# Splitting the streamed weights of a hybrid layer by DMA instead of by ScalarE and VectorE

## The chip, the cores and the metric

The kernel runs on one NeuronCore of one Trainium2 chip. The metric is the device time of one execution in microseconds (us); the lower, the better. The kernel before takes 900.84 us, the median of 3 runs (900.33 to 902.33).

## The reference, cut to what matters

One decoder layer on 512 tokens of width 1024, all in float32: RMSNorm, one wide input projection, four mixer branches (a short gated convolution, causal pooling, a 31-tap convolution, differential attention), each gated by a sigmoid and summed, an output projection, and a gated feed-forward part of inner width 2816.

```python
h = rms_norm(x, mix_norm)
z = h @ w_in
sc_b, sc_c, sc_x, pool_in, conf_in, q, k, v, gate_logits = split(z)
y = [short_conv(...) @ sc_out, pool_mixer(...), conformer(...) @ conf_out, diff_attention(...) @ diff_out]
x = x + sum_i(sigmoid(gate_i) * y_i) @ w_o
h2 = rms_norm(x, ffn_norm)
u = causal_dwconv(h2 @ w_up, conv_w)          # 2 x 2816 channels
x = x + (silu(gate(u)) * up(u)) @ w_down
```

Nearly all the arithmetic is products of an activation with a weight, and each weight is used once, for all 512 tokens.

## The kernel before

**Precision.** TensorE multiplies in the type F32R, which keeps fewer bits than F32. So every operand is written as a pair: `hi`, the value rounded to F32R, and `lo = value - hi`, rounded too. `mm3` makes one product out of three matmuls (lines 134 to 136): hi with hi, hi of the first with lo of the second, lo of the first with hi of the second. In `project` the first is the weight.

**The stream of weights.** All weights lie in HBM as one array `w` of 155 chunks of 128 x 1024 F32 (512 KB) in the order in which they are used. A chunk holds 8 units, a unit being a 128 x 128 block. Each call of `unit` hands out the next unit, lets work run that was put off by so many units (`events`), and calls `load_chunk` until chunk c + AHEAD is there (AHEAD = 2).

**Loading a chunk.** `fetch` issues a DMA on SP's queue into `raw`, of which there are two buffers. Then ScalarE copies `raw` to `hi` with a cast (L108) and VectorE subtracts `hi` from `raw` into `lo` (L109). There are three buffers each of `hi` (`whi`) and `lo` (`wlo`). A buffer comes free when the last matmul that reads it is done. The first chunk is split in 4 pieces, the second in 2.

**Order.** The program is written with tiles, and a planner puts the instructions of each engine in order: of those whose inputs it reckons ready it takes the one written first. Each engine, and each queue that issues DMAs, then works strictly in the order given, and an instruction that waits holds up those behind it. Only for the first two chunks is the order of ScalarE and VectorE the written one (`manual_schedule`).

**The other work.** GpSimd sums squares of the input (L207), raises to the power -1/2 (L249, L348), clears the padding of tiles (L85) and adds up the pooling windows (L491). It issues no DMA. VectorE and ScalarE do all that reads PSUM: norms, convolutions, softmax, gates, and the split of activations. Eight PSUM banks hold the results of the projections until then. `at_` are two buffers of the attention part, used again by the feed-forward part.

Of the kernel before, what the change touches and what calls it, by code (L numbers as in the profile page):

```python
# [9 lines left out]
F32 = mybir.dt.float32  # L10
F32R = mybir.dt.float32r
AF = mybir.ActivationFunctionType
ALU = mybir.AluOpType
AX = mybir.AxisListType

P = 128
T = 512
# [10 lines left out]
CW = 1024  # L28
TW = T + CK - 1
UPC = CW // P  # L30
AHEAD = 2
STEP = 13
TAP0 = 32
TAP1 = 560
# [8 lines left out]
HP = 0  # L43
# [20 lines left out]
def hybrid_layer_kernel(ctx: ExitStack, tc: tile.TileContext, xT: bass.AP, w: bass.AP, cols: bass.AP, out: bass.AP):  # L64
    nc = tc.nc
    const = ctx.enter_context(tc.tile_pool(name="const", bufs=1))
    big = ctx.enter_context(tc.tile_pool(name="big", bufs=1))
    wp = ctx.enter_context(tc.tile_pool(name="wp", bufs=3))
# [19 lines left out]
    chunks = []  # L88
# [2 lines left out]
    early = []  # L91

    def fetch(c, pieces=1):
        raw = wp.tile([P, CW], F32, tag="raw", name=f"wr{c}", bufs=2)
        for i in range(pieces):
            s = slice(i * CW // pieces, (i + 1) * CW // pieces)
            nc.sync.dma_start(raw[:, s], w[c][:, s])
        return raw

    def load_chunk(pieces=1):  # L100
        c = len(chunks)
        raw = early.pop(0) if early else fetch(c)
        hi = wp.tile([P, CW], F32R, tag="whi", name=f"wh{c}", bufs=3)
        lo = wp.tile([P, CW], F32R, tag="wlo", name=f"wl{c}", bufs=3)
        with tc.high_priority(HP):
            for i in range(pieces):
                s = slice(i * CW // pieces, (i + 1) * CW // pieces)
                nc.scalar.copy(hi[:, s], raw[:, s])  # L108
                nc.vector.tensor_tensor(out=lo[:, s], in0=raw[:, s], in1=hi[:, s].bitcast(F32), op=ALU.subtract)  # L109
        chunks.append((hi, lo))  # L110
# [11 lines left out]
    def unit(width=1):  # L122
        u = state["unit"]
        state["unit"] += width
        while events and events[0][0] <= u:
            events.pop(0)[2]()
        c, o = divmod(u, UPC)
        while len(chunks) <= min(c + AHEAD, n_chunks - 1):
            load_chunk()
        s = slice(o * P, (o + width) * P)  # L130
        return chunks[c][0][:, s], chunks[c][1][:, s]
# [48 lines left out]
    nc.scalar.copy(ones, ones32)  # L180
    xin = [big.tile([P, 4, T], F32, tag=f"od{i}", name=f"xin{i}") for i in range(2)]
    hs = big.tile([P, KD, 2, T], F32R, name="hs")
    at_ = [big.tile([P, 4, T], F32R, name=f"at{i}") for i in range(2)]
    xt = [xin[k // 4][:, k % 4, :] for k in range(KD)]
    raw = []
    total = const.tile([P, T], F32, name="total")
# [4 lines left out]
    nc.sync.dma_start(xt[0], xT[0])  # L191
    nc.sync.dma_start(gains, cols[:, :NG])
    early.append(fetch(0, 2))
    nc.sync.dma_start(xt[1], xT[1])
    early.append(fetch(1))
    nc.sync.dma_start(xin[0][:, 2:4, :], xT[2:4].rearrange("k p t -> p k t"))
    nc.sync.dma_start(xin[1], xT[4:8].rearrange("k p t -> p k t"))
# [11 lines left out]
    with tc.manual_schedule(engines={mybir.EngineType.Activation, mybir.EngineType.DVE}):  # L209
        raw_in(0)  # L210
        load_chunk(PIECES)
        raw_in(1)
        load_chunk(2)
        for k in range(2):
            add_square(total, xt[k], k == 0, f"sq{k}", nc.gpsimd)
# [179 lines left out]
    nc.scalar.activation(lam2, lam2, AF.Exp)  # L395
    nc.vector.tensor_tensor(out=lam, in0=lam2[:, 0:1], in1=lam2[:, 1:2], op=ALU.subtract)
    nc.vector.tensor_scalar(out=lam, in0=lam, scalar1=LAM_INIT, scalar2=None, op0=ALU.add)

    def scores(i, hd):
        n = (i + 1) * P  # L400
        qs = slice(i * P, n)
        sc = [bank(f"sc{i}{hd}{m}") for m in range(2)]
        for a, b, s0, s1 in ((0, 0, True, False), (0, 1, False, False), (1, 0, False, True)):
            for m in range(2):
                r = slice(m * HD, (m + 1) * HD)
                nc.tensor.matmul(sc[m][:, :n], qT[hd][a][r, qs], kT[hd][b][r, :n], start=s0, stop=s1)
        st = sm.tile([P, 4], F32, tag="st", name=f"st{i}{hd}")
        ps = []
        for m in range(2):
            p = t2(f"p{i}{hd}{m}")  # L410
            nc.vector.tensor_tensor_reduce(  # L411
                out=p[:, :n], in0=sc[m][:, :n], in1=mask[:, T - n:], scale=-1.0, scalar=-NEG, op0=ALU.add, op1=ALU.min,
                accum_out=st[:, m:m + 1])
            nc.scalar.activation(  # L414
                p[:, :n], p[:, :n], AF.Exp, bias=st[:, m:m + 1], scale=-1.0, accum_out=st[:, 2 + m:3 + m])
            ps.append(p)
        nc.vector.reciprocal(st[:, 2:4], st[:, 2:4])
        nc.vector.tensor_tensor(out=st[:, 3:4], in0=st[:, 3:4], in1=lam, op=ALU.mult)
        nc.scalar.activation(ps[1][:, :n], ps[1][:, :n], AF.Copy, scale=st[:, 3:4])
        nc.vector.scalar_tensor_tensor(  # L420
            out=ps[0][:, :n], in0=ps[0][:, :n], scalar=st[:, 2:3], in1=ps[1][:, :n],
            op0=ALU.mult, op1=ALU.subtract)
        after(LAG, lambda: values(i, hd, ps[0]))
# [307 lines left out]
```

## Time and profile before

| what | value |
|---|---|
| runs, median (lowest to highest) | 900.84 us (900.33 to 902.33) |
| profiled execution, first to last instruction | 899.2 us |
| PE busy | 890.3 us, 99% |
| PEld (weight loads) busy | 725.8 us, 81% |
| VectorE (DVE) busy | 592.2 us, 66% |
| ScalarE (ACT) busy | 387.3 us, 43% |
| GpSimd (POOL) busy | 47.9 us, 5% |
| HBM read | 85.75 MB, 98 GB/s with what is written |

For the profiled execution the profile gives the span, not a time of its own beside it: 899.2 us from the first to the last instruction, 1.6 us under the median of the runs. That difference is taken as what lies around the span. Matmuls are pipelined, so how close PE is to its limit is read from the distance between the starts of its matmuls and not from its busy share.

### The profile page before, as it was taken

How to read it: one execution, taken by the hardware profiler on the slowest of the kernel's cores; microseconds unless marked ns; L12 is line 12 of the kernel's file. 1: busy time of each engine (PE TensorE's matmuls, PEld its weight loads, DVE VectorE, ACT ScalarE, POOL GpSimd, SP SyncE). 2: the span in 40 equal slices, each digit the busy share in tenths (PEclk: the TensorE clock that was granted, in tenths of full speed). 3: DMA queues.
4: the chain of work that ended last, by engine and by line, in shares of the span. 5: the costliest groups of instructions: out<-in, count | busy, mean ns of one | idle time of the engine just before them, and what ended most of it. 6: DMA issues, size and time to landing. Idle time of an engine off the chain costs nothing.

```text
span 899.2 us, 10320 instructions
## 1 busy us (share of the span) xinstructions
PE 890.3 (99%) x3974; PEld 725.8 (81%) x3974; DVE 592.2 (66%) x853; ACT 387.3 (43%) x544; POOL 47.9 (5%) x108
## 2 busy tenths in 40 slices
PE   7999999999999999999999999999999999999998
PEld 5888887778787888888888888888888888888886
DVE  6599855998575999743558555877777777632221
ACT  6333454464588352222574346444444444311110
POOL 5003300002400000000000000000000000000000
PEclk9999999999999999999999999999999999999999
DMA  5423222222132222222334332322223322233330
GB/s 199 141 90 99 71 93 94 71 71 95 47 110 78 94 94 94 93 94 94 96 96 159 135 99 72 117 94 95 94 94 101 107 97 94 94 117 106 117 105 24
DMA packets 26337, 88.51 MB, mean 98 GB/s; under 512 B 2992, under 2 KB 3248, under 8 KB 26288
## 3 DMA queue, kind: packets, MB, share of 16 engines
q1 hardware_dynamic: 26288, 87.86, 29.3%
q8 instruction: 31, 0.51, 0.2%
q14 instruction: 18, 0.15, 0.1%
HBM read 85.75 MB, written 2.10 MB: 98 GB/s over the span
## 4 chain that ended last, share of the span: by engine, by line
PE 92%; DVE 4%; ACT 2%; issue 1%; DMA 1%; SPq 0%; DVEq 0%; ACTq 0%
PE dn L135 4%; PE dn L136 4%; PE dn L134 4%; PE fg L134 4%; PE fu L134 4%; PE fg L136 4%; PE fu L136 4%; PE fg L135 4%; PE fu L135 4%; PE gts L134 2%; PE wo L134 2%; PE wo L136 2%; PE wo L135 2%; PE gts L135 2%; PE gts L136 2%; PE gtp L134 2%
## 5 line engine op out<-in xcount | busy, mean ns | idle before, releaser
L109 DVE TENSOR_TENSOR wl<-wr,wh 128x1024 fp32r<-128x1024 f32 (+1 forms) x159 | 192.8, 1216 | 134.5 <-ACT wh L108 126.9
L108 ACT CAST wh<-wr 128x1024 fp32r<-128x1024 f32 (+1 forms) x159 | 163.3, 1030 | 261.9 <-PE dn L135 80.2
L324 DVE SCALAR_TENSOR_TENSOR cacc<-glu,colt,cacc 128x512 f32<-128x512 f32 x120 | 89.2, 755 | 1.6
L134 PE MATMUL fg<-hs,wh 128*128 128x512 f32 x176 | 68.5, 389 | 0.0
L136 PE MATMUL fg<-hs,wl 128*128 128x512 f32 x176 | 68.5, 389 | 0.0
L136 PE MATMUL fu<-hs,wl 128*128 128x512 f32 x176 | 68.5, 389 | 0.0
L135 PE MATMUL fg<-hs,wh 128*128 128x512 f32 x176 | 68.5, 389 | 0.0
L134 PE MATMUL fu<-hs,wh 128*128 128x512 f32 x176 | 68.5, 389 | 0.0
L135 PE MATMUL fu<-hs,wh 128*128 128x512 f32 x176 | 68.5, 389 | 0.0
L611 DVE SCALAR_TENSOR_TENSOR fc<-f,colt,fc 128x512 f32<-128x512 f32 x88 | 65.8, 749 | 1.4
L136 PEld LDWEIGHTS fu<-hs,wl 128*128 128x128 f32 x176 | 33.1, 188 | 6.9
L134 PEld LDWEIGHTS fg<-hs,wh 128*128 128x128 f32 x176 | 33.1, 188 | 6.9
L135 PEld LDWEIGHTS fu<-hs,wh 128*128 128x128 f32 x176 | 33.0, 188 | 6.9
L136 PEld LDWEIGHTS fg<-hs,wl 128*128 128x128 f32 x176 | 33.0, 187 | 6.9
L135 PEld LDWEIGHTS fg<-hs,wh 128*128 128x128 f32 x176 | 33.0, 188 | 6.8
L134 PEld LDWEIGHTS fu<-hs,wh 128*128 128x128 f32 x176 | 33.0, 187 | 6.8
L606 DVE TENSOR_TENSOR f<-fu,rs 128x512 f32<-128x512 f32 x22 | 15.2, 692 | 34.5 <-PE fu L136 34.5
L609 ACT ACTIVATE fc<-f,colt 128x512 f32<-128x512 f32 x44 | 31.9, 726 | 4.8 <-DVE f L606 4.6
L85 POOL MEMSET f<- 128x2 f32 x44 | 4.4, 100 | 507.1 <-DVE total L207 292.7
L624 ACT ACTIVATE fc<-fc 128x512 f32<-128x512 f32 x22 | 13.9, 634 | 38.7 <-DVE fc L611 38.7
L414 ACT ACTIVATE p<-p,st 128x128 f32<-128x128 f32 (+3 forms) x32 | 17.8, 556 | 29.6 <-DVE st L411 29.6
L134 PE MATMUL gts<-hs,wh 128*128 128x512 f32 x64 | 26.0, 406 | 0.0
(920 smaller groups left out, 2099.6 us busy)
## 6 DMA issues: line engine op xcount, KB each, us to landing
wr<-w SPq DMA_DIRECT2D x154, 512.0 KB, 3.3
x<-xT SPq DMA_DIRECT2D x8, 256.0 KB, 5.0
outT<-out SPq DMA_DIRECT2D x7, 256.0 KB, 2.6
xin<-xT SPq DMA_DIRECT2D x1, 1024.0 KB, 9.2
xin<-xT SPq DMA_DIRECT2D x2, 256.0 KB, 4.0
wr<-w SPq DMA_DIRECT2D x2, 256.0 KB, 3.7
xin<-xT SPq DMA_DIRECT2D x1, 512.0 KB, 7.0
colt<-cols SPq DMA_DIRECT2D x1, 273.5 KB, 9.4
```

Of the source, the lines that this page charges most:

```text
L85: nc.gpsimd.memset(t[:, :n], 0.0)
L108: nc.scalar.copy(hi[:, s], raw[:, s])
L109: nc.vector.tensor_tensor(out=lo[:, s], in0=raw[:, s], in1=hi[:, s].bitcast(F32), op=ALU.subtract)
L134: nc.tensor.matmul(ps, a[0], b[0], start=start, stop=False)
L135: nc.tensor.matmul(ps, a[0], b[1], start=False, stop=False)
L136: nc.tensor.matmul(ps, a[1], b[0], start=False, stop=stop)
L324: nc.vector.scalar_tensor_tensor(out=acc31[j], in0=glus[j][:, i:i + T], scalar=wc, in1=acc31[j], op0=ALU.mult, op1=ALU.add)
L414: nc.scalar.activation(p[:, :n], p[:, :n], AF.Exp, bias=st[:, m:m + 1], scale=-1.0, accum_out=st[:, 2 + m:3 + m])
L606: nc.vector.tensor_tensor(out=u[:, 2:2 + T], in0=ps, in1=rs, op=ALU.mult)
L609: nc.scalar.activation(c, u[:, 2:2 + T], AF.Copy, scale=col("ffn_conv", o + 2))
L611: nc.vector.scalar_tensor_tensor(out=c, in0=u[:, i:i + T], scalar=col("ffn_conv", o + i), in1=c, op0=ALU.mult, op1=ALU.add)
L624: nc.scalar.activation(g, g, AF.Silu)
```

## The change

Chunks 0 to 3 are loaded as before. From chunk 4 on (`ENGINES = 4`) three steps make the pair, without a raw copy in SBUF:

- a DMA issued by GpSimd writes the chunk from HBM into `hi`, with a cast to F32R on the way;
- ScalarE writes `-hi` into the tile `lo`;
- a second DMA issued by GpSimd reads the chunk from HBM again and adds it onto `lo`.

AHEAD becomes 3, and there are four buffers each of `hi` and `lo`. The `raw` buffers of the first four chunks lie in the memory of `at_`, which is allocated later.

```diff
-AHEAD = 2
+AHEAD = 3
+ENGINES = 4
...
     def fetch(c, pieces=1):
-        raw = wp.tile([P, CW], F32, tag="raw", name=f"wr{c}", bufs=2)
+        raw = big.tile([P, 2, CW], F32, tag=f"at{c % 2}", name=f"wr{c}")[:, 0, :]
...
+    def weight_pair(c):
+        return tuple(wp.tile([P, CW], F32R, tag=f"w{x}", name=f"w{x[0]}{c}", bufs=4) for x in ("hi", "lo"))
+
+    def split_by_dma(c):
+        hi, lo = weight_pair(c)
+        nc.gpsimd.dma_start(hi, w[c])
+        with tc.high_priority(HP):
+            nc.scalar.activation(lo, hi.bitcast(F32), AF.Copy, scale=-1.0)
+        nc.gpsimd.dma_start(lo, w[c], accum_op=ALU.add)
+        return hi, lo
+
     def load_chunk(pieces=1):
         c = len(chunks)
+        if c >= ENGINES:
+            chunks.append(split_by_dma(c))
+            return
         raw = early.pop(0) if early else fetch(c)
-        hi = wp.tile([P, CW], F32R, tag="whi", name=f"wh{c}", bufs=3)
-        lo = wp.tile([P, CW], F32R, tag="wlo", name=f"wl{c}", bufs=3)
+        hi, lo = weight_pair(c)
...
-    at_ = [big.tile([P, 4, T], F32R, name=f"at{i}") for i in range(2)]
...
+    at_ = [big.tile([P, 4, T], F32R, tag=f"at{i}", name=f"at{i}") for i in range(2)]
```

The pair holds the same values in both kernels, up to the rounding of the last step.

## Rows read from the trace of the kernel before

**Rows 1.** Page, part 1: busy us (share of the span) x instructions.

```profile
PE 890.3 (99%) x3974; PEld 725.8 (81%) x3974; DVE 592.2 (66%) x853; ACT 387.3 (43%) x544; POOL 47.9 (5%) x108
```

**Rows 2.** Waits of PE: for what, us in total, times, longest us.

```profile
PE ca L136 <- DVE wl L109: 2.8, 1, 2.8
PE warm L202 <- DVE zeros L199: 1.4, 1, 1.4
PE ca L134 <- ACT wh L108: 0.5, 1, 0.5
PE os L450 <- DVE oq1l L160: 0.2, 1, 0.2
```

**Rows 3.** Timeline of PE in the feed-forward part, eight units apart: start, duration, instruction.

```profile
599.63 0.39 PE L134 MATMUL fu<-hs,wh 128*128 128x512 f32 x1
...
605.07 0.39 PE L134 MATMUL fg<-hs,wh 128*128 128x512 f32 x1
```

**Rows 4.** Timeline of PE: a gap, chunk 4's first; chain of waits: the last add.

```profile
19.24 0.40 PE L135 MATMUL ca<-raw4l,wh 128*128 128x512 f32 x1
22.41 0.96 PE L136 MATMUL ca<-raw4h,wl 128*128 128x512 f32 x3 [2.77 <-DVE wl L109]
...
33.12 0.48 PE L134 MATMUL pa<-raw0h,wh 128*128 128x512 f32 x1
...
895.42 0.42 DVE out L636
```

**Rows 5.** Page, part 5, the split of weights: busy us, mean ns, idle before.

```profile
L109 DVE TENSOR_TENSOR wl<-wr,wh 128x1024 fp32r<-128x1024 f32 (+1 forms) x159 | 192.8, 1216 | 134.5 <-ACT wh L108 126.9
L108 ACT CAST wh<-wr 128x1024 fp32r<-128x1024 f32 (+1 forms) x159 | 163.3, 1030 | 261.9 <-PE dn L135 80.2
```

**Rows 6.** The line of the chunks' DMAs: issue ns min/median/max, and time to landing.

```profile
L97 SPq DMA_DIRECT2D wr<-w x156: 327/328/432, 1.6 to 870.1; - x156
...
DMA to landing us min/median/max: 3.0/3.3/8.1
```

**Rows 7.** Page, part 3: SP's queue: packets, MB, share of 16 engines' span.

```profile
q1 hardware_dynamic: 26288, 87.86, 29.3%
```

**Rows 8.** Waits of SP's queue, the longest.

```profile
SPq L97 <- DVE wl L109: 737.9, 147, 13.4
```

**Rows 9.** GpSimd's instructions by line: busy us, mean ns, idle before.

```profile
L348 POOL TENSOR_TENSOR qss<-qss,half 128x8 f32<-128x8 f32 x4 | 7.3, 1853 | 44.8 <-DVE qss L346 44.8
...
L249 POOL TENSOR_TENSOR r1r<-r1v,half 128x4 f32<-128x4 f32 x1 | 1.0, 1020 | 10.0 <-DVE r1v L247 10.0
```

**Rows 10.** GpSimd's timeline: two rows of the start, two of the pooling part.

```profile
0.87 0.10 POOL L221 MEMSET epsc<- 128x1 f32 x1
...
11.47 12.02 POOL L207 TENSOR_TENSOR total<-total,sq 128x512 f32<-128x512 f32 x7 [8.51 <-ACT sq L205]
...
210.89 1.62 POOL L491 TENSOR_TENSOR ps<-px 128x527 f32<-128x527 f32 x1 [13.15 <-ACT px L486]
...
235.65 4.07 POOL L491 TENSOR_TENSOR ps<-ps 128x525 f32<-128x525 f32 x3
```

**Rows 11.** Waits of ACT from 130 to 310 us, the longest.

```profile
ACT p L414 <- DVE st L411: 29.6, 14, 4.7
```

**Rows 12.** By stretch: busy us (x) of PE, PEld, DVE, ACT, POOL; clock; DMA share; GB/s.

```profile
130.00:200.00 70.00, 70.00 (x331) 55.44 (x329) 53.05 (x107) 35.95 (x69) 0.31 (x3) 1.00 0.24 83
200.00:240.00 40.00, 39.74 (x191) 31.18 (x190) 30.99 (x59) 17.59 (x35) 13.78 (x13) 1.00 0.25 79
...
500.00:750.00 250.00, 250.00 (x1102) 206.41 (x1101) 179.60 (x228) 115.03 (x147) 4.31 (x43) 1.00 0.29 97
780.00:880.00 100.00, 100.00 (x438) 81.96 (x438) 26.60 (x26) 19.86 (x19) 0.00 (x0) 1.00 0.31 106
```

## The prediction

> **What bounds the kernel now.** I read the busy shares first: PE is busy for 890.3 of 899.2 us, VectorE for two thirds, GpSimd for 5% [rows 1]. Since matmuls overlap, the share alone proves little, so I went on to the starts. In the feed-forward part eight units, that is one chunk or 24 matmuls, start from 599.63 to 605.07: 5.44 us, 0.227 us a matmul, with no gap [rows 3]. The waits of PE are the third view: 2.8 us for the low part of a chunk, 1.4 us before the warm-up, 0.5 and 0.2 us, 4.9 us in all [rows 2]. So PE sets the pace from end to end, and nearly nothing waits ahead of it. The granted clock is full (1.00, the 2.4 GHz level) in every stretch shown [rows 12]. From the first matmul of chunk 4 at 33.12 to the last output add at 895.42 [rows 4] are 862.3 us for the 151 chunks that the change touches: 5.71 us a chunk on average, 5.44 where PE does nothing else.
>
> The reader should see from this that the change works on engines that don't set the time. It can win a few us where PE waits, and it loses whatever its new chain fails to deliver every 5.44 us.
>
> **What is removed.** VectorE loses 151 subtractions of 1.216 us, 184 us of its 592 [rows 1, 5]. PE waits for one of these in a place that matters, once, for 2.8 us [rows 2], and that one belongs to chunk 2 (raw4 is unit 16 and up), which VectorE still splits. So this is worth 0 on the path; what hides it is PE's own work. SP loses 151 issues of 0.33 us [rows 6], and its wait for VectorE to free `raw` (737.9 us in all [rows 8]), also worth 0, since chunks lie ready ahead of PE. ScalarE keeps one pass over each chunk. I price the negation as the cast it replaces, 1.03 us [rows 5]: 0 again.
>
> **What is added.** Per chunk GpSimd issues two DMAs. Before, it issues none, so three prices aren't in the trace.
>
> - *The issue itself.* From below SP's issue, 0.33 us [rows 6]; from above GpSimd's dearest small instruction, 1.85 us, with 1.02 for the cheapest that computes [rows 9]. I take 1.0, that of a small program on the engine that has to do it. Two per chunk are 2.0 us of 5.44, beside 48 us of other work in the whole kernel [rows 1]. From either end the engine fits (0.7 to 3.7 us a chunk).
> - *The casting DMA.* SP's queue moved 87.86 MB in 29.3% of 899.2 us on all 16 engines [rows 7]: 263 us, 3.0 us per MB, 1.57 us for a chunk of 0.524 MB. That is my price if the cast is free; nothing cheaper is possible for the same bytes. From above, the worst landing of a chunk, 8.1 us [rows 6].
> - *The accumulating DMA.* It has to fetch the old content of `lo` besides the weight, so two reads for each write. From below again 1.57 us, from above 8.1. I take twice the copy, 3.1 us, as reads set the pace if both come through the same engine.
>
> The Trainium skill says the same of a DMA that adds ("Collectives: The Full Stack", section "The bandwidth ceiling: the fold count and why AG ≠ RS ≠ AR"): it needs two source reads and runs at half the rate of a copy. No row here shows it; an estimate by that page is 3.1 us too.
>
> The sum per chunk on the DMA engines is 1.57 + 3.1 = 4.7 us of 5.44, 86% in the dense stretches, where it was 0.29 to 0.31 before [rows 12]. It fits, with 0.8 us to spare: this is the tightest place of the whole change. From the bounds it is 3.1 to 16.2 us a chunk.
>
> **The latency of a chunk.** With four buffers, chunk c + 4 takes the place of c, so its first DMA waits until PE has read c for the last time, and PE needs c + 4 three chunks later, after 3 x 5.44 = 16.3 us. The chain in between: issue 1.0, landing 3.3 [rows 6], ScalarE 1.03 after whatever stands before it, issue 1.0, landing 3.3 plus the 1.57 that the second read adds: 11.2 us. That leaves 5.1 us. In the score stage ScalarE stands still up to 4.7 us for VectorE, 14 times [rows 11], and GpSimd has a block of 4.07 us of pooling sums and a wait of 13.15 us before another [rows 10]; each alone fits barely or falls into the planner's order.
>
> **What else waits on GpSimd.** The adds of the input norm (11.5 to 23.5 us), the powers, the paddings and the pooling sums now stand in one queue with DMAs that wait for PE or ScalarE. The adds end 9.6 us before chunk 4 starts [rows 4, 10], and the paddings are asked for well before PE would run out of its eight banks. I cost this at 0; without the cover it is some us per place.
>
> **The start.** Chunks 2 and 3 are still split by the engines, and the 2.8 us gap before 22.41 [rows 4] is VectorE finishing chunk 2 behind the splits of the input. AHEAD = 3 only brings chunk 3 forward. I take 0; the bounds are -2.8 (gap closed) and +2.8 (chunk 3 taking VectorE's time from the input in the same way).
>
> **The sum.** 899.2 us of span, plus 0 for PE's work, 0 for VectorE, SP and ScalarE, 0 at the start, plus the 1.6 us by which the median of the runs lies over the span: 900.8 us. Differences under 0.2% (1.8 us) can't be told from no change in this kernel.
>
> **The rivals.** Each steady rival has a lap time p per chunk, and from rows 4 the total is 33.1 + 151 p + 3.8 + 1.6 = 38.5 + 151 p; p = 5.71 gives back 900.7.
>
> - *The DMA engines become the bound.* If the cast isn't free, or the add costs over 2.5 copies, the two transfers exceed 5.44 us. With three copies' worth p is 1.57 + 4.7 = 6.3 and the time 990 us; it decides from 3.87 us for the add on. For it: 86% by my own sum, and no row of such a DMA. Against: 3.0 us per MB is a price from engines that were idle for 70% of the time [rows 7]; with more queued they may move more per us. Chance 0.24.
> - *GpSimd's queue turns latency into pace.* A strict order cast, add, cast, add makes each cast wait until ScalarE has negated the chunk before. The planner does reorder GpSimd: the padding constant of L221 ran at 0.87 us, before the add of L207 that is written earlier and ran at 11.47 [rows 10]. But by rows the add is ready 3.3 + 1.03 = 4.3 us after the cast, sooner than the next buffer comes free (5.44), so the planner may well choose just that order. The lap is then 4.3 plus an issue of 0.33 to 1.0, 4.7 to 5.4 us, if the add of the chunk before leaves the engines free, and up to 3.1 more if it doesn't: 8.5. Halfway, p = 6.6 and 1035 us. It decides from a lap of 5.44. Chance 0.18. The Trainium skill speaks against the change here ("DMA: Bandwidth & Descriptors", section "Latency and other measured facts"): a DMA generated in software on GpSimd delivers its first byte after about 1 us, one generated in hardware after about 0.6. No row here shows the former; an estimate with 0.4 us more is p = 7.0 and 1095 us.
> - *Local stalls.* Where ScalarE's waits of up to 4.7 us and GpSimd's blocks of 4 meet the 5.1 us to spare, from about 30 to 310 us, PE waits now and then. Two to five times some 2 to 4 us is +4 to +20, about 911 us. Chance 0.16.
> - *Faster.* The gap at the start closes, since the planner places the chunks anew: 900.8 - 2.8 = 898.0 us. For it: it is the one wait of size that PE has. Against: the chunk concerned is split as before. Chance 0.12.
>
> **How the numbers follow.** That the new chain keeps up and nothing changes has 0.30, the largest single chance, so the predicted time is 900.8 us, with 899.0 to 902.6 as its own range. Faster has 0.12, and slower 0.24 + 0.18 + 0.16 = 0.58, spread over three mechanisms with different times. The range of 8 in 10 goes from 897 to 1060 us: no change and faster (0.41 of 0.42), local stalls (0.16), about 0.15 of the DMA bound (p up to 6.77) and half of the queue's (0.08), 0.80 in all.
>
> **What the profile after would show.** If I am right, PE's waits stay near 5 us, matmuls start every 0.227 us, VectorE is near 408 us busy, the DMA share is 0.8 or more in the feed-forward part, and the casts are issued as soon as PE frees a buffer. A DMA share at 1.0 with PE waiting for the add shows the first rival; PE waiting at a DMA share well under 1, with GpSimd's queue alternating strictly and waiting for ScalarE, the second; waits of PE confined to the part before 310 us, the third. What would make the forecast wrong first is the price of the accumulating DMA, for which I have only the copy.

## The result, and the profile after

The changed kernel takes 1062.11 us (median of 4 runs, 1060.18 to 1065.03) where the kernel before takes 900.92: a ratio of 1.178, 95% interval 1.175 to 1.181. It is slower, and the forecast of 900.8 us is missed, also by the range, which ended at 1060.

The page of the profiled execution (span 1058.5 us), first its busy times, then its DMA queues and its issues with the median time to landing:

```profile
PE 942.4 (89%) x3974; PEld 744.1 (70%) x3974; DVE 419.4 (40%) x702; ACT 380.3 (36%) x544; POOL 259.8 (25%) x410
...
q0 software_dynamic: 43488, 158.35, 65.2%
q1 hardware_dynamic: 4544, 8.68, 2.3%
...
wh<-w POOLq DMA_DIRECT2D x151, 512.0 KB, 6.6
wl<-w POOLq DMA_DIRECT2D x151, 512.0 KB, 5.4
```

PE is idle for 116 us where it was idle for 9 [rows 1]. VectorE has lost 173 us of work, as the change says, and nothing comes of it. The DMA engines read nearly twice the bytes (164.9 MB, 85.75 before) and are still busy for only two thirds of the time, so they aren't full. GpSimd is at 25%, not full either. Where a kernel is slower by 18% and no engine is full, engines wait for each other, and the waits show which. Who waited for whom, us in total, times, longest:

```profile
POOL wl L109 <- ACT wl L108: 693.8, 137, 11.6
ACT wl L108 <- DMA wh<-w: 417.5, 94, 9.1
...
PE fu L150 <- DMA wl<-w: 18.1, 14, 3.0
PE dn L150 <- DMA wl<-w: 15.2, 8, 2.8
PE os L464 <- ACT oq1h L173: 8.5, 1, 8.5
```

L106 is the casting DMA, L108 ScalarE's negation, L109 the accumulating DMA. GpSimd stands at the add and waits for ScalarE, ScalarE waits for the cast to land, and PE waits for the add: 70 us of its waits are for `wl`, 42 for ScalarE and VectorE. The timeline of GpSimd, and then of ScalarE, over one turn of this circle (start, duration, instruction, idle time before it and its releaser):

```profile
179.29 0.85 POOL L109 DMA_DIRECT2D wl<-w  x1 [6.49 <-ACT wl L108]
179.84 0.87 POOL L106 DMA_DIRECT2D wh<-w  x1
180.38 0.44 POOL L86 MEMSET u<- 128x2 f32 x1
187.86 0.85 POOL L109 DMA_DIRECT2D wl<-w  x1 [7.04 <-ACT wl L108]
188.40 0.87 POOL L106 DMA_DIRECT2D wh<-w  x1
...
186.50 1.06 ACT L108 ACTIVATE wl<-wh 128x1024 fp32r<-128x1024 f32 x1 [4.45 <-DMA wh<-w]
```

The cast goes out at 179.84, right behind the add of the chunk before (179.29). The negation starts at 186.50, 6.66 us later, and takes 1.06. The add starts at 187.86 and the next cast at 188.40: 8.56 us from cast to cast, where PE uses up a chunk in 5.44 [rows 3]. The next cast stands behind the add in the queue, so it can't go out early although the DMA engines have room. In GpSimd's timeline this order, add of c ahead of the cast of c + 1, holds for 99 of the 150 chunks that have another behind them; for the other 51 the cast is ahead.

ScalarE's queue is held up in the same way. Its negation waits for the cast, and the work of the attention part stands behind it. The longest wait of PE, the 8.5 us above, ends with such a piece (L173):

```profile
277.30 1.06 ACT L108 ACTIVATE wl<-wh 128x1024 fp32r<-128x1024 f32 x1 [3.42 <-DMA wh<-w]
...
279.44 0.62 ACT L173 CAST oq1h<-oq 128x512 fp32r<-128x512 f32 x1
```

In the kernel with the order pinned and the cast first, below, no wait of PE for ScalarE is longer than 0.9 us.

By stretch, busy us of PE, PEld, DVE, ACT, POOL, then clock, DMA share and GB/s, for the feed-forward part:

```profile
500.00:750.00 250.00, 221.68 (x924) 175.45 (x923) 96.11 (x143) 100.22 (x133) 56.99 (x95) 0.97 0.72 169
```

924 matmuls in 250 us where there were 1102 [rows 12], at a DMA share of 0.72. The granted clock, 1.00 before, is 0.97: part of the time PE runs at the lower level (1.2 GHz) after it has stood still.

### The profile page after: what moved, and what is told of

Its sections match the earlier page's. It is cut to its first block, busy times and chain, and to the rows that moved or that the text cites. A ratio compares the mean times of both kernels' runs of the same rounds, so it can differ in the third digit from the quotient of the medians.

```text
span 1058.5 us, 10397 instructions
## 1 busy us (share of the span) xinstructions
PE 942.4 (89%) x3974; PEld 744.1 (70%) x3974; DVE 419.4 (40%) x702; ACT 380.3 (36%) x544; POOL 259.8 (25%) x410
## 3 DMA queue, kind: packets, MB, share of 16 engines
q0 software_dynamic: 43488, 158.35, 65.2%
## 4 chain that ended last, share of the span: by engine, by line
issue 31%; DMA 10%; POOL 8%; PE 2%; ACT 2%; DVE 0%; POOLq 0%; DVEq 0%; ACTq 0%
DMA wh<-w 8%; POOL wh L106 4%; POOL wl L109 3%; DMA wl<-w 2%; POOL f L86 1%; ACT wl L108 1%; PE dn L150 0%; PE dn L148 0%; PE dn L149 0%; PE gtc L150 0%; PE gtc L148 0%; PE wo L150 0%; PE gtc L149 0%; ACT sgc L533 0%; PE wo L148 0%
## 5 line engine op out<-in xcount | busy, mean ns | idle before, releaser
L108 ACT ACTIVATE wl<-wh 128x1024 fp32r<-128x1024 f32 x151 | 159.7, 1057 | 524.1 <-DMA wh<-w 417.5
L109 POOL DMA_DIRECT2D wl<-w x151 | 132.1, 875 | 750.1 <-ACT wl L108 693.8
L106 POOL DMA_DIRECT2D wh<-w x151 | 117.1, 846 | 22.8 <-PE ca L150 7.7
L150 PE MATMUL fu<-hs,wl 128*128 128x512 f32 x176 | 72.2, 410 | 18.1 <-DMA wl<-w 18.1
L148 PE MATMUL fu<-hs,wh 128*128 128x512 f32 x176 | 70.3, 400 | 0.0
L149 PE MATMUL fu<-hs,wh 128*128 128x512 f32 x176 | 70.3, 399 | 0.0
L651 DVE TENSOR_TENSOR out<-dn,x 128x512 f32<-128x512 f32 (+1 forms) x9 | 5.6, 631 | 127.5 <-PE dn L150 127.5
L149 PEld LDWEIGHTS fu<-hs,wh 128*128 128x128 f32 x176 | 34.0, 193 | 7.6
L148 PEld LDWEIGHTS fu<-hs,wh 128*128 128x128 f32 x176 | 34.2, 194 | 6.8
L539 DVE TENSOR_TENSOR sgd<-yd,sgd 128x512 f32<-128x512 f32 x8 | 5.5, 692 | 65.2 <-ACT sgd L533 65.2
L150 PE MATMUL gtc<-hs,wl 128*128 128x512 f32 x64 | 26.0, 407 | 4.1 <-DMA wl<-w 4.0
L150 PE MATMUL gtp<-hs,wl 128*128 128x512 f32 x64 | 26.3, 410 | 2.5 <-DMA wl<-w 2.5
```

Source lines behind the costliest of these rows:

```text
L106: nc.gpsimd.dma_start(hi, w[c])
L108: nc.scalar.activation(lo, hi.bitcast(F32), AF.Copy, scale=-1.0)
L109: nc.gpsimd.dma_start(lo, w[c], accum_op=ALU.add)
L148: nc.tensor.matmul(ps, a[0], b[0], start=start, stop=False)
L149: nc.tensor.matmul(ps, a[0], b[1], start=False, stop=False)
L150: nc.tensor.matmul(ps, a[1], b[0], start=False, stop=stop)
```

## The experiments

**The theory** is that latency becomes pace: cast, landing, negation, add and next cast follow each other, because GpSimd's queue has them in this order. **The rival** is that the transfers themselves, with the add's second read, are more than the DMA engines can move in 5.44 us. The first four kernels keep the two apart.

**Order pinned, cast first.** The add of chunk c is issued behind the cast of chunk c + 1. Nothing else differs.

```diff
+    held = []
     def split_by_dma(c):
         hi, lo = weight_pair(c)
-        nc.gpsimd.dma_start(hi, w[c])
+        d = nc.gpsimd.dma_start(hi, w[c])
+        if held:
+            with tc.issue_after(d.ins):
+                nc.gpsimd.dma_start(held[0][0], held[0][1], accum_op=ALU.add)
         with tc.high_priority(HP):
             nc.scalar.activation(lo, hi.bitcast(F32), AF.Copy, scale=-1.0)
-        nc.gpsimd.dma_start(lo, w[c], accum_op=ALU.add)
+        held[:] = [(lo, w[c])]
+        if c == n_chunks - 1:
+            nc.gpsimd.dma_start(lo, w[c], accum_op=ALU.add)
```

> Same transfers, same ScalarE pass; only the order on GpSimd's queue is pinned: the add of chunk c stands behind the cast of chunk c + 1, always. Queue theory (the lap is latency, since in 100 of 151 cases the add of c stands ahead of the cast of c + 1): the cast goes out as soon as PE frees its buffer, the lap falls to PE's own 5.44 us and the time to 900 to 915 us. Rival, DMA-engine theory (the two transfers together cost more than PE's 5.44 us): the order doesn't matter, 1040 to 1065 us.

Measured: 907.0 us, 1.0051 of the kernel before (1.0033 to 1.0069). Its timeline of GpSimd (L108 the cast, L111 the add), and its software queue on the page, with a larger share since the same transfers fall into less time:

```profile
839.50 0.55 POOL L108 DMA_DIRECT2D wh<-w  x1 [3.03 <-PE dn L157]
840.12 0.85 POOL L111 DMA_DIRECT2D wl<-w  x1
844.95 0.55 POOL L108 DMA_DIRECT2D wh<-w  x1 [3.97 <-PE dn L157]
847.54 0.86 POOL L111 DMA_DIRECT2D wl<-w  x1 [2.05 <-ACT wl L113]
850.50 0.55 POOL L108 DMA_DIRECT2D wh<-w  x1 [2.09 <-PE dn L157]
...
q0 software_dynamic: 43488, 158.35, 81.7%
```

The cast now waits for PE and goes out every 5.5 us; PE leads and the queue follows. All the transfers of the changed kernel fit into a span of 903.9 us. The rival falls.

**Order pinned, add first.** The same two DMAs, strictly alternating.

```diff
...
+        if last:
+            with tc.issue_after(last[0].ins):
+                nc.gpsimd.dma_start(hi, w[c])
...
-        nc.gpsimd.dma_start(lo, w[c], accum_op=ALU.add)
+        last[:] = [nc.gpsimd.dma_start(lo, w[c], accum_op=ALU.add)]
```

> The order on GpSimd's queue is pinned the other way: cast, add, cast, add for all chunks, where the changed kernel has the next cast ahead of the add in 51 of 151 cases. Queue theory: every lap is that of the strictly alternating stretch of the changed kernel, some 8.0 us (cast issued at 171.93, the next at 179.84), so 38.5 + 151 x 8.0 = 1247 us. DMA-engine theory: nothing changes, 1050 to 1075 us.

Measured: 1279.96 us in one run. GpSimd's timeline (L110 the cast, L115 the add):

```profile
1104.54 0.86 POOL L115 DMA_DIRECT2D wl<-w  x1 [6.52 <-ACT wl L114]
1105.09 0.86 POOL L110 DMA_DIRECT2D wh<-w  x1
1112.62 0.87 POOL L115 DMA_DIRECT2D wl<-w  x1 [6.66 <-ACT wl L114]
1113.16 0.88 POOL L110 DMA_DIRECT2D wh<-w  x1
1120.92 0.86 POOL L115 DMA_DIRECT2D wl<-w  x1 [6.88 <-ACT wl L114]
```

8.1 and 8.3 us from add to add, a little over the 8.0 expected. With 8.2 the formula of the prediction gives 38.5 + 151 x 8.2 = 1277 us. The order alone, with the same work on every engine, moves the time from 907 to 1280 us; the changed kernel lies between, being a mixture.

**Chain cut.** ScalarE writes zeros instead of the negative, so the add needn't wait for the cast.

```diff
+    zcol = const.tile([P, 1], F32, name="zcol")
+    nc.gpsimd.memset(zcol, 0.0)
...
-            nc.scalar.activation(lo, hi.bitcast(F32), AF.Copy, scale=-1.0)
+            nc.scalar.activation(lo, zcol.broadcast_to([P, CW]), AF.Copy, scale=-1.0)
```

> ScalarE writes zeros into the low tile instead of the negative of the high part, so it no longer waits for the cast; both DMAs (the second still accumulating), the pass on ScalarE and the buffers stay. The low tile then holds the whole weight, so this part of the result differs. Queue theory: the add no longer hangs on the landing of the cast, both go out when a buffer is free, 900 to 915 us. DMA-engine theory: the same bytes with the same adds, 1040 to 1065 us.

Measured: 898.71 us, 0.9955 (0.9937 to 0.9972), below what I expected. GpSimd's timeline (L109 the cast, L112 the add):

```profile
843.23 0.56 POOL L109 DMA_DIRECT2D wh<-w  x1 [3.37 <-PE dn L153]
844.55 0.86 POOL L112 DMA_DIRECT2D wl<-w  x1 [0.76 <-ACT wl L111]
848.73 0.56 POOL L109 DMA_DIRECT2D wh<-w  x1 [3.32 <-PE dn L153]
```

Here too the add stands ahead of the next cast, for 149 of 150 chunks, and it costs nothing: the add goes out 1.3 us after its cast, and the next cast waits for PE. So the order by itself isn't the cause, nor is the wait for the cast by itself, which the kernel with the cast first has too; the two together are. The theory holds.

The 4 us below the kernel before needed an explanation of their own. About half come from the start: chunk 4's first matmul is at 31.24 us here, at 33.12 before [rows 4] and at 36.38 in the kernel with the cast first. The rest goes with the granted clock: it is 1.000 in all four runs here, and 0.996 to 0.998 in 11 of the 14 runs of the kernel before beside them (spans of 900.3 to 902.6 us; 898.9 to 899.3 in the other three).

**The cast alone.** The kernel before, with the high part by the casting DMA; `raw` and VectorE's subtraction stay.

```diff
+ENGINES = 4
...
+        if c >= ENGINES:
+            nc.gpsimd.dma_start(hi, w[c])
...
-                nc.scalar.copy(hi[:, s], raw[:, s])
+                if c < ENGINES:
+                    nc.scalar.copy(hi[:, s], raw[:, s])
```

> The kernel before with one part of the change: from chunk 4 on the high part comes by GpSimd's casting DMA instead of ScalarE's copy; raw still comes by SP's queue and VectorE still subtracts. Two plain reads per chunk, nothing on GpSimd's queue waits for ScalarE. Queue theory: 899 to 903 us, as before. Theory that a casting DMA or GpSimd's issue is itself too slow: over 920 us.

Measured: 901.95 us, 0.9995 (0.9985 to 1.0004): no difference. Its queues (GpSimd's casts, SP's plain copies) and landings on the page:

```profile
q0 software_dynamic: 21744, 79.18, 28.1%
q1 hardware_dynamic: 26288, 87.86, 28.1%
...
wr<-w SPq DMA_DIRECT2D x154, 512.0 KB, 4.2
wh<-w POOLq DMA_DIRECT2D x151, 512.0 KB, 4.1
```

28.1% of 901.1 us are 253 us, so a cast takes 1.68 us of the 16 engines, and it lands no later than a plain copy beside it. The kernel with the cast first spends 81.7% of 903.9 us, 739 us, on casts and adds; less the 253 the add takes 485 / 151 = 3.2 us. By the changed kernel's own page, 65.2% of 1058.5 us, it is 2.9. Both are estimates, as they take the cast to cost the same beside adds.

**The add without adding.** The second DMA only writes; order and waits as in the changed kernel.

```diff
-        nc.gpsimd.dma_start(lo, w[c], accum_op=ALU.add)
+        nc.gpsimd.dma_start(lo, w[c])
```

> The changed kernel with one word less: the second DMA of a chunk no longer accumulates but writes the weight over the negative, after the same wait for ScalarE and in the same order on GpSimd's queue. The low tile then holds the whole weight, so this part of the result differs. If the lap is the cast's landing behind the transfer ahead of it, then with half the reads ahead of it the cast lands after 5 us instead of 6.6, the lap falls by some 1.6 us to about 5.4 and the time to 900 to 935 us. If the add's reads don't hold up the cast, the landing and the time stay within 2% of the changed kernel.

Measured: 910.12 us in one run. The order on GpSimd's queue is the same, 99 adds ahead and 51 casts ahead. The line of its casts:

```profile
L106 POOL DMA_DIRECT2D wh<-w x151: 530/537/711, 19.6 to 883.5; - x151
...
DMA to landing us min/median/max: 3.4/4.5/8.6
```

The cast lands after 4.5 us instead of 6.6 when what was issued ahead of it reads half as much. GpSimd's issue of the second DMA is shorter too, 0.53 us instead of 0.87, a smaller part. So the add's length belongs to the cause: it doesn't fill the engines, it stands in front of the one transfer on which the circle waits.

**The start.** In every kernel so far GpSimd adds up squares from 11 us on, mostly until 23, while VectorE splits the input and chunks 2 and 3. Moving these seven adds to VectorE was tried on two kernels (the same edit in two places):

```diff
-            add_square(total, xt[k], k == 0, f"sq{k}", nc.gpsimd)
+            add_square(total, xt[k], k == 0, f"sq{k}")
```

> The kernel with each cast ahead of the add before it, and the seven adds of the input norm moved from GpSimd to VectorE. Theory for what is left of its loss (4.7 us of span, 3.3 of it before chunk 4): GpSimd's adds slow VectorE's instructions with two inputs in SBUF down (2.2 to 2.7 us for a subtraction that takes 1.22 alone), PE waits 3.6 us for chunk 2 and then runs at a granted clock of 0.59 to 0.73 for up to 10 us. Without these adds on GpSimd the gap falls under 1 us, the clock stays at 1.00 and the span falls by 4 to 6 us, to 898 to 900, the runs to 900 to 902. Rival (the loss is the DMAs' traffic at the start): no change, 906 to 908.

> The kernel before with the same move alone: the seven adds of the input norm on VectorE. If the gap at the start is the two engines in each other's way, it is gone here too, and the time is 2 to 4 us under the kernel before, whatever splits the weights: 897 to 899. Rival (the gain in the kernel with zeros for the negative came from its DMAs): 900 to 903, as before.

Measured: with the cast first 902.13 us, 0.9998 (0.9985 to 1.0011); the kernel before with this edit alone 898.06 us, 0.9961 (0.9946 to 0.9975), which is faster than both kernels of this study. VectorE's timeline at this place, first with the cast first and GpSimd adding (L130), then the kernel before with the adds moved (L109):

```profile
19.84 5.36 DVE L130 TENSOR_TENSOR wl<-wr,wh 128x1024 fp32r<-128x1024 f32 x2
```

```profile
18.50 1.22 DVE L109 TENSOR_TENSOR wl<-wr,wh 128x1024 fp32r<-128x1024 f32 x1
19.63 0.69 DVE L207 TENSOR_TENSOR total<-total,sq 128x512 f32<-128x512 f32 x1
20.24 1.23 DVE L109 TENSOR_TENSOR wl<-wr,wh 128x1024 fp32r<-128x1024 f32 x1
```

Two subtractions take 5.36 us beside GpSimd's adds and 1.22 and 1.23 without. In the kernel with zeros GpSimd issues DMAs just then, and the next of its adds (L223) comes later, so that two subtractions (L126) take 2.35 us:

```profile
19.45 2.35 DVE L126 TENSOR_TENSOR wl<-wr,wh 128x1024 fp32r<-128x1024 f32 x2
...
20.21 1.82 POOL L112 DMA_DIRECT2D wl<-w  x2
21.72 1.65 POOL L223 TENSOR_TENSOR total<-total,sq 128x512 f32<-128x512 f32 x1
```

So its gain at the start was not its transfers'. My number for the cast-first kernel with the adds moved, 900 to 902, was just missed, though the gap is gone as foretold: its start is as early as that of the kernel before with the edit (chunk 4's first matmul at 30.88 and 30.85 us), but its profiled execution ends 2.7 us later, with three waits of PE for adds, of 1.5, 0.7 and 0.7 us, such as this:

```profile
PE fu L157 <- DMA wl<-w: 1.5, 1, 1.5
```

The three add up to 2.9 us, about the whole difference. So even with the best order found, the change brings nothing that the kernel before doesn't have with the same edit.

## Why the prediction was wrong

**What bounds the kernel before** was right: PE does, and the work that VectorE is spared is worth 0. It is at 419 us (408 foretold), and no part of the 173 us saved shows in the time.

**The prices** were right. The cast costs 1.68 us of the DMA engines (1.57 foretold), the add 2.9 to 3.2 (3.1), GpSimd's issue mostly 0.53 to 0.88 us (1.0). Cast and add are 4.9 us at most and fit into 5.44: the cast-first kernel shows it at 907 us. The add takes 1.7 to 1.9 times the cast. The Trainium skill ("Collectives: The Full Stack", section "The bandwidth ceiling: the fold count and why AG ≠ RS ≠ AR") says of the adding step of a collective that it needs two source reads and so runs at half the rate of the copying step; the add of this case agrees with that roughly.

**The step that failed is the latency of a chunk.** I set its sum against the time of three chunks (11.2 us against 16.3), as if the chains of neighbouring chunks ran side by side. They share GpSimd's queue, and in it the next chunk's first DMA mostly stands behind this chunk's second. Then not the sum has to fit into three chunks, but one turn of the circle into one: 8.2 us in the strict order, against 5.44. The landing of 3.3 us in that sum was also wrong: it is a row of a queue with one reader, and in the changed kernel, behind adds, the median is 6.6. The 0 for ScalarE failed with it: its pass costs what was said (1.06 us), but it now stands waiting in front of the attention part's work, and PE waits 25 us for ScalarE in all, where it was 0.5 [rows 2].

The mechanism is that of the second rival, and its strict form, 8.5 us at the upper bound, is measured at 8.2. That its 1035 us came near to 1062 is partly luck. Its lap of 6.6 us was halfway between two bounds for one order; the measured (1062.1 - 38.5) / 151 = 6.78 comes from a mixture of two orders, which by themselves take 8.2 and about 5.5.

**The chance of 0.18 was the error of judgement.** The rows that speak for the strict order stand in the prediction, and I still weighed the circle below the undisturbed case. What the planner reckons inside isn't shown by any run, nor why it put 51 casts ahead; the order that came out is shown. (The constant of L221, which the prediction calls one of the padding, is the epsilon of the norms. That the planner moved it ahead is read rightly.)

**The other rivals.** The DMA engines were not the bound. The local stalls exist (after the start 0.7 to 1.5 us each in the last kernel with the cast first) but are small. The gap at the start could be closed, worth 0.4% in the kernel before, yet by an edit that has nothing to do with how weights are split; in the changed kernel it is wider (3.6 us of waiting instead of 2.8).

**Where the loss lies.** The span is 159 us longer. PE's idle time has grown by 116 - 9 = 107 of them, and PE is busy 52 us longer for the same matmuls. The mean granted clock of 0.957 is worth up to 46 us of 1058.5; how the 52 divide is not shown.

The Trainium skill's later first byte of a DMA generated on GpSimd ("DMA: Bandwidth & Descriptors", section "Latency and other measured facts") can't be read here, as the profile has landings and not first bytes; in the landings of whole chunks nothing of it shows: in the same kernel the casts land after 4.1 us and SP's copies after 4.2.

## What to carry to other kernels

When two DMAs of one tile are issued by the same engine and the second waits for work on the first, ask what stands behind the second in that queue: if it is the next tile's first DMA, the whole latency has to fit into the time in which one tile is used up, however empty the engines are. Issue the next tile's first DMA ahead of this tile's second, and price a landing with what was issued just before it, not from an idle queue. And before work is taken off an engine, check that PE ever waits for that work; here it waited 2.8 us of 899 for VectorE's split of weights.

## What the runs showed of the hardware that was not expected

VectorE's instructions with two inputs in SBUF take longer beside GpSimd's adds of two tiles in SBUF: the subtraction takes 1.22 us alone and 2.2 to 2.7 us beside the adds. The Trainium skill says so ("SBUF — State Buffer", section "Who interferes with whom"): a VectorE instruction with two SBUF inputs contends with a GpSimd instruction that reads SBUF. The runs agree, and without it the kernel before is 0.4% faster: 3.6 us, of which some 2 are left against those of its runs whose granted clock was 0.999 or 1.000. GpSimd's adds hardly suffer: 1.7 us each beside VectorE's work, 1.6 us for one without in the kernel with zeros.

A gap of PE of 2.8 us at the start of the kernel before left the granted clock at 1.00. One of 3.6 us in the cast-first kernel went with a lower clock, and so did one of 3.0 us in the kernel with the cast alone (0.64 and 0.68 in the two stretches below). But one of 3.6 us in the kernel with the plain second DMA left it at 1.00, so the length of a gap alone doesn't decide; what does is not shown. By stretch, in the columns as above, first with the cast first, then with the plain second DMA:

```profile
20.00:25.00 5.00, 1.97 (x5) 1.59 (x6) 5.00 (x2) 1.55 (x2) 4.38 (x5) 0.73 0.60 210
25.00:30.00 5.00, 5.00 (x15) 3.92 (x14) 0.85 (x2) 0.57 (x1) 0.53 (x1) 0.59 0.65 108
```

```profile
20.00:25.00 5.00, 1.67 (x7) 1.40 (x8) 5.00 (x3) 1.44 (x3) 4.39 (x5) 1.00 0.64 210
25.00:30.00 5.00, 5.00 (x23) 4.05 (x23) 1.17 (x2) 0.89 (x1) 1.58 (x3) 1.00 0.51 153
```

15 matmuls in 5 us instead of 23: after the same gap the lower clock costs about 2 us in this stretch, more than the 0.8 us by which the gap is longer than in the kernel before.
